# A hybrid diffusion layer on one core: fewer constant matmuls, the second row between the first tiles, filter transfers on another queue, filter steps ahead of the columns

## The chip, the cores and the metric

The kernel runs on one NeuronCore of a Trainium2 chip. A core has five engines that run side by side, each with its own queue, in order: TensorE (PE, matrix multiply, its weight loads shown apart as PEld), VectorE (DVE), ScalarE (ACT), GpSimd (POOL) and SyncE (SP, which here only starts DMA transfers). Matmuls write to PSUM; everything else lies in SBUF. The metric is the device time of one execution in microseconds, lower is better, as the median of several runs. The profile and the trace come from one more, profiled execution.

## The reference, cut to what matters

One layer over 256 latent tokens and 256 context tokens of width 2048, all in float32:

```python
mod   = (silu(c)     @ w_ada + b_ada)      # 9 chunks of 2048: shift, scale, gate for three sub-layers
mod_c = (silu(c_ctx) @ w_ada + b_ada)
x   = half_ffn(x,   mod,   0, g0, w_up1, w_dn1)    # x + 0.5 * gate * swiglu(rms_norm(x) * (1+scale) + shift)
ctx = half_ffn(ctx, mod_c, 0, g0, w_up1, w_dn1)
h, hc = modulated norms of x, ctx                  # then one input projection
attn = attention(q, [kc; k], [vc; v])              # 8 query heads, 2 key heads
hyo  = hyena(h @ w_hy, filters)                    # short conv, gate, long convolution by rfft/irfft, gate
x = x + gate * (concat(rms_norm(attn), rms_norm(hyo)) @ w_out)
x = half_ffn(x, mod, 2, g2, w_up2, w_dn2)
```

The long filter of the Hyena group depends on weights alone: a small three-layer sine network over 256 positions, `h = sin(freq * (z @ w + b))` three times, then `h @ w4` times `exp(-t * abs(decay))`, forward and backward halves, normalised by the sum of absolute values, and its Fourier transform.

## The kernel before, in words

Tokens lie along the free axis: `xs[i]` holds stream i (0 latent, 1 context) as 16 blocks of 128 features by 256 tokens. A matmul in float32 accuracy is made of three faster ones: each operand is split in a high part `hi` (ACT, a cast) and a low part `lo` (DVE, the difference), and `mm3` (L231 to L234) adds hi x hi, lo x hi and hi x lo. `Ffn.tile` does this for one block k of features and one feed-forward tile j of 128 gate and 128 up columns: six matmuls of 128x512.

The change lies in the start of the program, before the main loop of the first feed-forward. It has these parts.

**Norm sums.** The 16 loads of x come first on SP's queue. ACT squares them (L594), DVE adds them up (L255), and PE sums over the features with matmuls against ones (L607, four matmuls of two columns each for a group). Around these stand constant matmuls, `keep_awake` (L578, `ones` times `pair`, 128x256, results unused): `AWAKE[0]` of them ahead of the first group of sums and `AWAKE[3]` between the first group and the rest. PE takes them in this order. Then follow the root (L262 to L271), a matmul that spreads the reciprocal root over the partitions (L297) and its copy into `rs`.

**Rows and columns of the conditioning.** Shift and scale of the first sub-layer are made for one block d of 128 features at a time. `row_load(d)` loads 2 MB of `w_ada1` as two tiles `wrow` of 1 MB (four buffers, so two rows); `ada_row(d)` is 16 matmuls of 256 columns (L175, 32 records in the trace); `ada_col(d)` copies the row to SBUF (ACT, L182, tile `sg`), turns it (PE, L184) and reduces it to a column (DVE, L187 to L190). Then `wave_h(d)` makes the modulated block `h[d]` in both parts: DVE L648, ACT L650 (hi), DVE L652 (lo); for d = 0 and 1 it is `wave_h_early` (DVE L628, ACT L635, DVE L638, L640).

**The wave.** As soon as `h[d]` is there, it is used for three feed-forward tiles at once (`WAVE = 3`, j = 0, 1, 2), which stay open in PSUM over all 16 blocks. A step d of the loop (L708) is: the row of block d+1, the tile of j = 0, the transposes of row d+1, the tiles of j = 1 and 2. The up weights of the wave come as 512 KB pieces of four blocks; `weights_on` (L686) casts the next pieces when d % 4 = 3 (L221, L225), and POOL's queue loads the ones after (L721 is a copy that gates them, L723 the loads). The first pieces are loaded in two slices, one block (`head`) and three blocks (`rest`), and cast by `first_hi` (ACT, L563) and `first_lo` (DVE, L566).

**Filter steps.** `filter_spectrum` is a generator; the wave calls `next(steps)` once a tile, and what is emitted there has its place in the order of every engine. Three sine layers (PE L436, DVE L438 to L443, ACT L445), then four quarters q of 256 channels. A quarter loads its *taps* (decay, L425, partition-broadcast, and `w4`, L428; 128 KB each, four DMAs), takes the absolute value (ACT L464), exponentials (L468), splits `w4` (ACT L470, DVE L471), multiplies (PE L475, L476), makes sums and norm (DVE L477 to L490, ACT L487, PE L493, L494, DVE L496), transforms (PE L502, DVE L503 to L508) and writes two *spectra* of 256 KB to DRAM (L510). Taps of quarter q+1 are loaded when quarter q begins. Before the change SP's queue carries the taps and the transform matrix (L450), among the rows, and ACT's queue the spectra.

The order of instructions within an engine is made when the program is built, from the order of the calls, their data and `then` / `issue_after`, which put one instruction behind another.

Of the kernel before, what the change touches and what calls it, by code (L numbers as in the profile page):

```python
# [33 lines left out]
FILTER_J = 36  # L34
GATE_J = 20

AWAKE = (32, 0, 0, 14)

QSTEP = (2, 1, 3, 2)
FILL = (2, 0)  # L40
# [15 lines left out]
def hybrid_layer_kernel(ctx: ExitStack, tc: tile.TileContext, a):  # L56
# [26 lines left out]
    def PB(shape=(P, 512)):  # L83
        return T(pp, shape, "pb")
# [327 lines left out]
    def filter_spectrum():  # L412
# [9 lines left out]
        def load_taps(q):  # L422
            dec, w4 = U((P, 2, L)), U((P, 2, L))
            for fb in range(2):
                nc.sync.dma_start(dec[:, fb, :],  # L425
                                  a["flt_decay"][:, fb * HW + q * L : fb * HW + (q + 1) * L].partition_broadcast(P))
            for r in range(2):
                nc.sync.dma_start(w4[r * NF : (r + 1) * NF],  # L428
                                  a["flt_w4"].rearrange("k (f c) -> k f c", f=2)[:, :, q * L : (q + 1) * L])
            return dec, w4  # L430


        for li in range(3):
            np_ = P if li == 2 else NF
            ps = PB((np_, L))
            PE.matmul(ps, ws[li], hcur, start=True, stop=True)  # L436
            ar, kk = T(up, (np_, L), "mt", bufs=3), T(up, (np_, L), "mt", bufs=3)
            V.tensor_scalar(ar, ps, vecs[0:np_, li : li + 1], vecs[0:np_, 3:4], op0=ALU.add, op1=ALU.mult)  # L438
            V.tensor_scalar(kk, ar, 1.0 / TWO_PI, MAGIC, op0=ALU.mult, op1=ALU.add)
            V.tensor_scalar(kk, kk, MAGIC, None, op0=ALU.subtract)  # L440
            for cst in (RED1, RED2, RED3):
                V.scalar_tensor_tensor(ar, kk, -cst, ar, op0=ALU.mult, op1=ALU.add)
            V.tensor_scalar(ar, ar, 3.1415925, -3.1415925, op0=ALU.min, op1=ALU.max)  # L443
            hcur = U((np_, L))
            S.activation(hcur, ar, AF.Sin)  # L445
            yield
            if li == 0:

                mats = U((P, 2, 2, P))
                nc.sync.dma_start(mats, a["fdft"])  # L450
            if li == 1:
                taps = [load_taps(0)]
            yield
            yield
# [4 lines left out]
        for q in range(4):  # L459
# [29 lines left out]
            V.tensor_add(kts[0], kts[0], kts[1])  # L489
            V.tensor_add(ab, ab, kts[0][:, 1, :])  # L490
            yield
            psn = PB((P, 2, L))
            PE.matmul(psn[:, 0, :], ones, ab, start=True, stop=True)  # L493
            PE.matmul(psn[0:1, 1, :], alt, pm[0][:, 0, :], start=True, stop=True)  # L494
# [4 lines left out]
            for sn in range(2):  # L499
                ps, eo, o = PB((P, 2, L)), kts[sn], now[sn]  # L500
                for t in range(2):
                    PE.matmul(ps[:, t, :], mats[:, sn, t, :], pm[t][:, sn, :], start=True, stop=True)  # L502
                V.tensor_mul(eo, ps, rn.unsqueeze(1).broadcast_to((P, 2, L)))  # L503
                V.tensor_add(o[:, 0, :], eo[:, 0, :], eo[:, 1, :])
                V.tensor_sub(o[:, 1, :], eo[:, sn, :], eo[:, 1 - sn, :])
                if sn:
                    V.tensor_copy(o[0:1, 0, :], now[0][0:1, 1, :])
                    V.tensor_copy(now[0][0:1, 1, :], mid)  # L508
                    for n in range(2):
                        nc.scalar.dma_start(spec[2 * q + n], now[n])  # L510
                yield


# [142 lines left out]


    wave = [f1.open(alt=j >= 2) for j in range(WAVE)]
    head, rest = slice(0, 1), slice(1, 4)
    then(roots[-1], first_hi, 0, head)  # L660
    with tc.issue_after(spread.ins):
        made = [first_hi(j, head) for j in range(1, WAVE)][-1]
# [25 lines left out]
            w[j] = weight(None, (P, 4, 2, P), raw=raws[j])  # L688


    for j in range(WAVE):
        mm = f1.tile(0, 0, w[j], wave[j]) if j == 0 else then(mm, f1.tile, 0, 0, w[j], wave[j])
    with tc.issue_after(shifted.ins), tc.issue_after(lo_last.ins):
        for j in range(2):
            first_hi(j, rest)
            first_lo(j, rest)
        scaled = times_rs(1)
    then(mm, row_on, 1)
    copied, mm, bank = then(scaled, ada_col, 1)
    shifted, lo_last = then(copied, wave_h_early, 1)  # L700
    with tc.issue_after(shifted.ins), tc.issue_after(lo_last.ins):
        first_hi(2, rest)
        first_lo(2, rest)
    with tc.issue_after(lo_last.ins), tc.issue_after(mm.ins):
        next(steps)
    mm = keep_awake(AWAKE[2], mm, bank)

    for d in range(1, KT):  # L708
        if d > 1:
            mm = then(mm, row_on, d + 1) or mm  # L710
        for j in range(WAVE):
            mm = then(mm, f1.tile, d, d % 4, w[j], wave[j])
            if d == 1 and j == 0:
                mm = then(mm, row_on, 2)
            if j == (1 if d == 1 else 0):
                mm = then(mm, col_on, d + 1) or mm
            weights_on(d, j)
            if (d, j) != (1, 0):
                next(steps, None)
        if d % 4 == 1 and d // 4 < 3:  # L720
            gate = G.tensor_copy(warm, mod[0][0][:, d : d + 1])  # L721
            with tc.issue_after(gate.ins):
                raws = [weight_load(f1.wup[j, d // 4 + 1], (P, 4, 2, P), G) for j in range(WAVE)]  # L723
# [719 lines left out]
```

## Time and profile before

| | us |
|---|---|
| median of 3 runs | 2686.22 |
| lowest and highest | 2685.14, 2686.62 |
| the profiled execution's own time | 2686.6 |
| its span (first to last instruction) | 2684.8 |
| granted clock of PE over the span | 0.993 |

| engine | busy us | share of the span |
|---|---|---|
| PE | 2654.8 | 99% |
| PE weight load | 2183.4 | 81% |
| DVE | 1725.7 | 64% |
| ACT | 940.5 | 35% |
| POOL | 6.4 | 0% |

How the rows of the trace are read: in a timeline row stand the start, the time taken, engine, line, operation, tiles (written <- read, without buffer numbers), shape and count, and in brackets how long the engine stood idle before it and what ended that. SPq, ACTq and POOL with `DMA_DIRECT2D` are the issuing of transfers, not the transfers. The granted clock is PE's: 1.00 is full speed, 0.50 half. A matmul's record overlaps the next, so the distance of two starts tells its price. In the list of DMA issues stand the tile, the queue, the count, the size of one and the median time from issue to landing.

### The profile page before, as it was taken

How to read it: one execution, taken by the hardware profiler on the slowest of the kernel's cores; microseconds unless marked ns; L12 is line 12 of the kernel's file. 1: busy time of each engine (PE TensorE's matmuls, PEld its weight loads, DVE VectorE, ACT ScalarE, POOL GpSimd, SP SyncE). 2: the span in 40 equal slices, each digit the busy share in tenths (PEclk: the TensorE clock that was granted, in tenths of full speed). 3: DMA queues.
4: the chain of work that ended last, by engine and by line, in shares of the span. 5: the costliest groups of instructions: out<-in, count | busy, mean ns of one | idle time of the engine just before them, and what ended most of it. 6: DMA issues, size and time to landing. Idle time of an engine off the chain costs nothing.

```text
span 2684.8 us, 32551 instructions
## 1 busy us (share of the span) xinstructions
PE 2654.8 (99%) x12538; PEld 2183.4 (81%) x12538; DVE 1725.7 (64%) x2700; ACT 940.5 (35%) x1238; POOL 6.4 (0%) x19
## 2 busy tenths in 40 slices
PE   9899999999999999999999999999999999999999
PEld 6568888888888888888888888888888888888887
DVE  4669898987587667542434497789765555554444
ACT  3343222222222222222222365457454444444333
POOL 0000000000000000000000000000000000000000
PEclk8899999999999999999999999999999999999999
DMA  8777656566687566633223355435545555556664
GB/s 313 251 286 236 226 209 219 210 229 210 226 276 258 204 229 210 224 120 101 95 95 101 126 169 183 144 110 164 197 160 190 190 188 188 188 189 207 200 203 157
DMA packets 145686, 515.77 MB, mean 192 GB/s; under 512 B 16699, under 2 KB 21756, under 8 KB 141180
## 3 DMA queue, kind: packets, MB, share of 16 engines
q1 hardware_dynamic: 142460, 504.13, 55.1%
q10 hardware_dynamic: 1776, 4.85, 0.5%
q0 software_dynamic: 1296, 4.72, 0.5%
q8 instruction: 98, 1.61, 0.2%
q14 instruction: 56, 0.46, 0.0%
HBM read 509.43 MB, written 4.21 MB: 191 GB/s over the span
## 4 chain that ended last, share of the span: by engine, by line
PE 97%; DVE 1%; ACT 1%; DMA 1%; issue 0%; SPq 0%; POOL 0%; DVEq 0%; ACTq 0%; POOLq 0%
PE pa L232 12%; PE pa L233 12%; PE pa L234 12%; PE pa L1107 10%; PE pa L1106 10%; PE pa L1105 10%; PE pb L232 7%; PE pb L233 7%; PE pb L234 7%; PE pa L240 3%; PE pa L242 2%; PE pb L175 1%; PE pa L819 1%; PE pa L820 1%; PE pa L818 1%; PE pa L578 1%
## 5 line engine op out<-in xcount | busy, mean ns | idle before, releaser
L225 DVE TENSOR_TENSOR wlo<-raw,whi 128x1024 fp32r<-128x1024 f32 x639 | 782.1, 1224 | 643.4 <-ACT whi L221 635.3
L221 ACT CAST whi<-raw 128x1024 fp32r<-128x1024 f32 x639 | 671.0, 1050 | 1338.8 <-PE pa L233 488.8
L232 PE MATMUL pa<-u,whi 128*128 128x512 f32 x1376 | 539.6, 393 | 3.2 <-ACT u L635 3.1
L233 PE MATMUL pa<-u,whi 128*128 128x512 f32 x1376 | 537.8, 391 | 0.4 <-DVE u L640 0.4
L234 PE MATMUL pa<-u,wlo 128*128 128x512 f32 x1376 | 537.1, 390 | 0.0
L1105 PE MATMUL pa<-whi,u 128*128 128x512 f32 x1060 | 414.1, 391 | 0.0
L1106 PE MATMUL pa<-wlo,u 128*128 128x512 f32 x1060 | 413.0, 390 | 0.2 <-DVE wlo L225 0.2
L1107 PE MATMUL pa<-whi,u 128*128 128x512 f32 x1060 | 413.0, 390 | 0.0
L232 PEld LDWEIGHTS pa<-u,whi 128*128 128x128 f32 x1376 | 258.9, 188 | 64.4 <-issue 6.9
L233 PEld LDWEIGHTS pa<-u,whi 128*128 128x128 f32 x1376 | 259.2, 188 | 55.1 <-DVE u L640 1.6
L234 PEld LDWEIGHTS pa<-u,wlo 128*128 128x128 f32 x1376 | 259.2, 188 | 53.9
L232 PE MATMUL pb<-u,whi 128*128 128x512 f32 (+1 forms) x800 | 298.8, 374 | 0.0
L233 PE MATMUL pb<-u,whi 128*128 128x512 f32 (+1 forms) x800 | 297.7, 372 | 0.0
L234 PE MATMUL pb<-u,wlo 128*128 128x512 f32 (+1 forms) x800 | 297.7, 372 | 0.0
L1106 PEld LDWEIGHTS pa<-wlo,u 128*128 128x128 f32 x1060 | 199.1, 188 | 41.4 <-DVE wlo L225 0.6
L1107 PEld LDWEIGHTS pa<-whi,u 128*128 128x128 f32 x1060 | 199.0, 188 | 41.4
L1105 PEld LDWEIGHTS pa<-whi,u 128*128 128x128 f32 x1060 | 199.1, 188 | 40.6
L138 DVE CUSTOM_DVE_ANT_0 adas<-adaw,crow,mod 128x1024 bf16<-128x1024 f32 x160 | 205.2, 1283 | 21.6 <-DMA adaw<-in_w_adaT_dram 18.9
L138 DVE CUSTOM_DVE_ANT_0 adas<-adaw,crow,cond 128x1024 bf16<-128x1024 f32 x160 | 205.0, 1281 | 16.4 <-DMA adaw<-in_w_adaT_dram 14.6
L232 PEld LDWEIGHTS pb<-u,whi 128*128 128x128 f32 x800 | 150.6, 188 | 27.2 <-issue 0.9
L233 PEld LDWEIGHTS pb<-u,whi 128*128 128x128 f32 x800 | 150.7, 188 | 26.3
L234 PEld LDWEIGHTS pb<-u,wlo 128*128 128x128 f32 x800 | 150.7, 188 | 26.2
(279 smaller groups left out, 2151.5 us busy)
## 6 DMA issues: line engine op xcount, KB each, us to landing
raw<-in_w_up_dram SPq DMA_DIRECT2D x340, 512.0 KB, 3.3
adaw<-in_w_adaT_dram SPq DMA_DIRECT2D x223, 512.0 KB, 4.9
raw<-in_w_dn_dram SPq DMA_DIRECT2D x184, 512.0 KB, 3.4
wrow<-in_w_ada_dram SPq DMA_DIRECT2D x32, 1024.0 KB, 7.3
raw<-in_w_hy_dram SPq DMA_DIRECT2D x32, 512.0 KB, 3.3
raw<-in_w_o_dram SPq DMA_DIRECT2D x32, 512.0 KB, 3.5
raw<-in_w_kv_dram SPq DMA_DIRECT2D x16, 512.0 KB, 3.3
raw<-in_w_q_dram SPq DMA_DIRECT2D x16, 512.0 KB, 3.3
```

The source lines that it names most:

```text
L138: V.tensor_tensor_reduce(out=sc, in0=t, in1=crow[i][:, b * (D // 2) : (b + 1) * (D // 2)], scale=1.0, scalar=mcol if b else bada[:, n : n ...
L175: last = PE.matmul(bank[g : g + 32, 0 : 2 * P], cs[:, k, :], t[:, k8, :], start=k < 4, stop=k >= KT - 4)
L221: S.copy(hi, raw)
L225: V.tensor_sub(lo, raw, hi.bitcast(F32))
L232: PE.matmul(ps, w[0], xx[0], start=start, stop=False)
L233: PE.matmul(ps, w[0], xx[1], start=False, stop=False)
L234: return PE.matmul(ps, w[1], xx[0], start=False, stop=stop)
L240: PE.matmul(ps, w[0], x, start=start, stop=stop)
L242: PE.matmul(ps[:, 0, :], w[1], x[:, 0, :], start=False, stop=False)
L1105: PE.matmul(ps[t], hi, w[0], start=start, stop=False)
L1106: PE.matmul(ps[t], hi, w[1], start=False, stop=False)
L1107: last = PE.matmul(ps[t], lo, w[0], start=False, stop=stop)
```

## The change

There are five edits.

1. The table of constant matmuls goes from (32, 0, 0, 14) to (17, 0, 0, 5): 17 ahead of the first sums, 5 between the two groups of sums. The call for the third number is taken out.
2. For d = 0 and 1 the order is written anew. Row 1 now comes after tile j = 0 of block 0, the transposes of row 1 after tile j = 1, and tile j = 2 after those; before, all three tiles came first. The weights' slices are one, one and two blocks (`head`, `second`, `rest`) in place of one and three, and the casts of `second` go between the column of row 1 and the modulation of block 1.
3. The taps and the transform matrix are issued from POOL's queue in place of SP's, and the spectra from POOL's in place of ACT's.
4. In a step of the wave `next(steps)` stands ahead of `col_on` and of `weights_on`, no more behind them.
5. A quarter of the filter has one more `yield`, ahead of its sums (the matmuls with `ones` and `alt`).

From line 489 on the new kernel's lines are one higher, and from the wave on six (L650 is then L651, L510 is L511, L721 is L727).

```diff
-AWAKE = (32, 0, 0, 14)
+AWAKE = (17, 0, 0, 5)
...
             for fb in range(2):
-                nc.sync.dma_start(dec[:, fb, :],
+                nc.gpsimd.dma_start(dec[:, fb, :],
...
             for r in range(2):
-                nc.sync.dma_start(w4[r * NF : (r + 1) * NF],
+                nc.gpsimd.dma_start(w4[r * NF : (r + 1) * NF],
...
-                nc.sync.dma_start(mats, a["fdft"])
+                nc.gpsimd.dma_start(mats, a["fdft"])
...
             V.tensor_add(ab, ab, kts[0][:, 1, :])
             yield
+            yield
             psn = PB((P, 2, L))
...
-                        nc.scalar.dma_start(spec[2 * q + n], now[n])
+                        nc.gpsimd.dma_start(spec[2 * q + n], now[n])
...
-    head, rest = slice(0, 1), slice(1, 4)
+    head, second, rest = slice(0, 1), slice(1, 2), slice(2, 4)
...
-    for j in range(WAVE):
-        mm = f1.tile(0, 0, w[j], wave[j]) if j == 0 else then(mm, f1.tile, 0, 0, w[j], wave[j])
+    scaled = then(lo_last, times_rs, 1)
+    mm = f1.tile(0, 0, w[0], wave[0])
+    mm = then(mm, row_on, 1)
+    mm = then(mm, f1.tile, 0, 0, w[1], wave[1])
+    with tc.issue_after(mm.ins), tc.issue_after(scaled.ins), tc.issue_after(shifted.ins):
+        copied, mm, _ = ada_col(1)
+    with tc.issue_after(copied.ins):
+        made = [first_hi(j, second) for j in range(2)][-1]
+    shifted, lo_last = then(made, wave_h_early, 1)
+    mm = then(mm, f1.tile, 0, 0, w[2], wave[2])
     with tc.issue_after(shifted.ins), tc.issue_after(lo_last.ins):
         for j in range(2):
-            first_hi(j, rest)
-            first_lo(j, rest)
-        scaled = times_rs(1)
-    then(mm, row_on, 1)
-    copied, mm, bank = then(scaled, ada_col, 1)
-    shifted, lo_last = then(copied, wave_h_early, 1)
-    with tc.issue_after(shifted.ins), tc.issue_after(lo_last.ins):
-        first_hi(2, rest)
-        first_lo(2, rest)
-    with tc.issue_after(lo_last.ins), tc.issue_after(mm.ins):
+            first_lo(j, second)
+        made = first_hi(2, second)
+        made_lo = first_lo(2, second)
+    for j in range(WAVE):
+        with tc.issue_after(made.ins), tc.issue_after(made_lo.ins):
+            made = first_hi(j, rest)
+            made_lo = first_lo(j, rest)
+    with tc.issue_after(made_lo.ins), tc.issue_after(mm.ins):
         next(steps)
-    mm = keep_awake(AWAKE[2], mm, bank)
...
+            if (d, j) != (1, 0):
+                next(steps, None)
             if j == (1 if d == 1 else 0):
                 mm = then(mm, col_on, d + 1) or mm
             weights_on(d, j)
-            if (d, j) != (1, 0):
-                next(steps, None)
```

What this makes of the instructions on the engines is shown at three places. The first is DVE at the third sine layer, which falls in step d = 3 of the wave. `pb_595` is the layer's matmul, `pb_628` the turned row of block 5; `wlo` are the low parts of the next weights. Before:

```order
L438 TENSOR_SCALAR mt_597<-pb_595,u_162 128x256
L225 TENSOR_TENSOR wlo_615<-raw_470,whi_614 128x1024
L439 TENSOR_SCALAR mt_598<-mt_597 128x256
L225 TENSOR_TENSOR wlo_625<-raw_472,whi_624 128x1024
L440 TENSOR_SCALAR mt_598<-mt_598 128x256
L442 SCALAR_TENSOR_TENSOR mt_597<-mt_598,mt_597 128x256
L187 TENSOR_REDUCE col_96<-pb_628 128x4
```

And now, where `pb_557` is the matmul and `pb_530` the turned row of block 4:

```order
L187 TENSOR_REDUCE col_96<-pb_530 128x4
L439 TENSOR_SCALAR mt_560<-mt_559 128x256
L188 SCALAR_TENSOR_TENSOR mod_6_83<-col_96,bada_17_95,cond_78 128x2
L440 TENSOR_SCALAR mt_560<-mt_560 128x256
L190 TENSOR_SCALAR mod_6_83<-col_96,cond_78 128x2
L442 SCALAR_TENSOR_TENSOR mt_559<-mt_560,mt_559 128x256
L649 SCALAR_TENSOR_TENSOR sq_579<-u_111,mod_6_83,u_166 128x256
```

The sine's chain has moved from behind the reduction of row 5 to beside that of row 4, one row earlier on DVE; the two weight differences that stood in it now follow it but for one.

The second place is ACT at the same step. `whi` are the casts of the three next weight pieces, u_582 (now u_577) is the high part of block 4, u_606 (now u_568) the third sine. Before:

```order
L221 CAST whi_591<-raw_468 128x1024
L650 ACTIVATE u_582<-sq_584,mod_6_83 128x256 x2
L221 CAST whi_614<-raw_470 128x1024
L464 ACTIVATE u_536<-u_536 128x512
L221 CAST whi_624<-raw_472 128x1024
L182 COPY sg_655<-pb_628 128x256
L445 ACTIVATE u_606<-mt_597 128x256
```

Now:

```order
L464 ACTIVATE u_518<-u_518 128x512
L221 CAST whi_586<-raw_450 128x1024
L221 CAST whi_596<-raw_452 128x1024
L221 CAST whi_606<-raw_454 128x1024
L445 ACTIVATE u_568<-mt_559 128x256
L651 ACTIVATE u_577<-sq_579,mod_6_83 128x256 x2
L457 CAST u_637<-u_568 128x256
L182 COPY sg_655<-pb_610 128x256
```

The high part of block 4 stood behind the first cast; it now stands behind all three casts and the sine. The copy of row 5 stood ahead of the sine and now stands behind it.

The third place is the queue of the spectra. On ACT, before, at the end of quarter 0 and the beginning of quarter 1 (u_674 and u_675 are the taps of quarter 1):

```order
L182 COPY sg_822<-pb_795 128x256
L650 ACTIVATE u_829<-sq_831,mod_6_83 128x256 x2
L510 DMA spec_20_100<-u_537 128x512
L510 DMA spec_19_99<-u_536 128x512
L468 ACTIVATE u_861<-u_674,u_162 128x512
L468 ACTIVATE u_863<-u_674,u_162 128x512
L470 CAST u_865<-u_675 128x512
L464 ACTIVATE u_854<-u_854 128x512
```

On POOL now, from the gate of the third set of weights to the spectra of quarter 2 (u_640 and u_641 are the taps, later the spectra, of quarter 1, u_1070 and u_1071 are the taps of quarter 3):

```order
L727 COPY mod_8_16_93<-mod_6_83 128x1
L209 DMA raw_1101<-in_w_up_dram 128x1024
L209 DMA raw_1103<-in_w_up_dram 128x1024
L209 DMA raw_1105<-in_w_up_dram 128x1024
L511 DMA spec_22_102<-u_641 128x512
L511 DMA spec_21_101<-u_640 128x512
L425 DMA u_1070<-in_flt_decay_dram 128x256 x2
L428 DMA u_1071<-in_flt_w_dram 64x2x256 x2
L511 DMA spec_24_104<-u_843 128x512
```

The spectra have left ACT, and on POOL the last taps stand behind the spectra of quarter 1.

## The prediction

> **What bounds the kernel now.** I read the windows of the trace by stage first, then the timeline of TensorE (PE) to the first feed-forward matmul, then PE's waits in the wave of 16 rows, then the queue that ended each.
>
> ```profile
> 0.00:36.59 36.59, 32.67 (x161) 25.14 (x161) 13.91 (x32) 15.77 (x29) 0.94 (x7) 0.91 0.86 323
> 36.59:50.99 14.40, 12.19 (x61) 7.28 (x61) 7.50 (x17) 3.58 (x6) 1.89 (x4) 0.77 0.50 185
> 50.99:187.50 136.51, 121.62 (x809) 78.07 (x808) 87.55 (x207) 47.92 (x84) 3.61 (x8) 0.91 0.78 287
> 187.50:2684.80 2497.30, 2488.32 (x11511) 2072.89 (x11510) 1616.77 (x2446) 873.26 (x1121) 0.00 (x0) 1.00 0.55 185
> ```
>
> Columns: stretch and length in us, busy time of PE, weight load, DVE, ACT and POOL, granted clock, DMA share, GB/s. From 187.5 us on PE works 2488.3 of 2497.3 us at full clock: no edit lies there, and it only starts earlier or later. The change can win only in the first 187.5 us. PE is busy in the first stretch too, but with what?
>
> ```profile
> 1.25 16.81 PE L578 MATMUL pa<-u,ones 128*128 128x256 f32 x64 [1.25 <-POOL u L91]
> 14.50 0.63 ACT L594 ACTIVATE u<-u 128x512 f32<-128x512 f32 x1 [0.70 <-DMA u<-in_xT_dram]
> 14.91 0.69 DVE L255 TENSOR_TENSOR u<-u 128x512 f32<-128x512 f32 x1
> 17.90 0.95 PE L607 MATMUL pb<-ones,u 128*128 128x2 f32 x8
> 18.71 6.29 PE L578 MATMUL pa<-u,ones 128*128 128x256 f32 x28
> 24.84 2.87 PE L607 MATMUL pb<-ones,u 128*128 128x2 f32 x24
> 27.74 0.16 DVE L262 TENSOR_SCALAR cond<-pb 128x4 f32<-128x4 f32 x1 [12.06 <-PE pb L607]
> 36.59 0.73 PE L232 MATMUL pa<-u,whi 128*128 128x512 f32 x2 [1.85 <-ACT u L635]
> ```
>
> The last squares are ready at 14.91 + 0.69 = 15.6 us, but the 24 records that sum them (L607) stand behind 28 records of constant matmuls and start at 24.84. DVE then waits 12.06 us for PE. Until 27.7 us the constant matmuls set the time.
>
> In the wave PE stands still four times, and each time the clock falls behind it:
>
> ```profile
> 77.00:80.56 3.56, 0.05 (x2) 0.01 (x1) 1.02 (x4) 3.53 (x7) 0.77 (x2) 1.00 1.03 287
> 80.56:85.98 5.42, 5.20 (x37) 2.14 (x37) 3.81 (x9) 1.74 (x3) 0.00 (x0) 0.69 0.96 379
> 99.50:102.81 3.31, 0.42 (x2) 0.00 (x1) 0.82 (x4) 1.89 (x4) 0.00 (x0) 0.94 1.01 314
> 102.81:109.28 6.47, 6.47 (x37) 2.53 (x37) 2.32 (x4) 0.48 (x1) 0.00 (x0) 0.51 0.23 66
> 113.90:119.14 5.24, 0.00 (x2) 0.00 (x1) 5.18 (x10) 2.40 (x4) 0.00 (x0) 0.70 0.08 33
> 119.14:123.80 4.66, 4.66 (x37) 2.14 (x37) 2.17 (x2) 0.00 (x0) 0.00 (x0) 0.60 0.01 4
> 153.90:156.09 2.19, 0.21 (x2) 0.00 (x1) 1.99 (x5) 2.19 (x5) 0.00 (x0) 1.00 1.05 431
> 156.09:162.47 6.38, 5.36 (x36) 2.00 (x37) 4.78 (x9) 1.53 (x2) 0.00 (x0) 0.57 0.96 327
> ```
>
> Standing: 3.51 + 2.89 + 5.24 + 1.98 + 1.02 = 14.6 us. Behind them, time x (1 - clock) is 5.42 x 0.31 + 6.47 x 0.49 + 4.66 x 0.40 + 5.36 x 0.43 = 9.0 us. Together 23.6 us of the 136.5 are lost to the filter steps' waits.
>
> **The constant matmuls (L578): 46 become 22.** 16.81 us / 32 = 0.53 us each in the first group (it begins cold), 6.29 / 14 = 0.45 in the second. The first group of 17 is 34 of 64 records. If the second group's 0.225 us a record is the warm price, the first has about 13 cold records of 0.44, and 34 take 5.7 + 21 x 0.22 = 10.3: it ends near 11.6 us. Eight sums (0.95) and five constant matmuls (2.25) end near 14.8, when the data are almost there (15.6). The 24 sums (2.87) then end at 17.7 instead of 27.7: **-10.0 us**. Bounds: -7.2 if the cold part is twice as long (26 records, so that the sums end at 20.5), -10.8 for 24 x 0.45.
>
> Is what follows ready 10 us earlier? Loads are issued by SP without waiting for PE until the third row, so their landings stand:
>
> ```profile
> L162 SPq DMA_DIRECT2D wrow<-in_w_ada_dram x1: 328/328/328, 10.4 to 10.4; - x1
> DMA to landing us min/median/max: 9.1/9.1/9.1
> ...
> L162 SPq DMA_DIRECT2D wrow<-in_w_ada_dram x1: 328/328/328, 13.8 to 13.8; - x1
> DMA to landing us min/median/max: 13.0/13.0/13.0
> ```
>
> Row 0's second half is in at 19.5 us. It is wanted behind L297, some 4 us after the sums, so near 21.8. Row 1 is in at 26.8 and wanted when tile j=0 ends, some 3 us after 26.6. Both have over 2 us to spare, so the chain from 27.7 to 36.59 moves whole.
>
> **Row 1 between the tiles.** No work is removed: the 32 records of row 1 go ahead of tile j=1, so that j=2 runs while the column is made. The lone wait is this one:
>
> ```profile
> 43.09 1.93 PE L175 MATMUL pb<-wrow,csp 128*32 128x256 f32 x32
> 47.81 1.22 PE L232 MATMUL pa<-u,whi 128*128 128x512 f32 x2 [1.28 <-ACT u L635]
> 50.99 1.36 PE L175 MATMUL pb<-wrow,csp 128*32 128x256 f32 x20
> ```
>
> The stretch 36.59 to 50.99 holds 14.40 - 12.19 = 2.2 us of idling. Tile j=2 (six matmuls, 1.4 us at 0.23) covers part. The slices cut into 1 + 1 + 2 k-tiles add three casts and three subtractions on engines that wait there. I take **-1.4 us**; bounds 0 and -2.2. The call with the table's third number goes too; that number was 0, so it made nothing.
>
> **Taps and spectra on POOL's queue.** What this takes away is ACT's wait for its own queue:
>
> ```profile
> 100.05 0.82 ACTq L510 DMA_DIRECT2D spec<-u  x2
> 100.92 1.33 ACT L468 ACTIVATE u<-u,u 128x512 f32<-128x512 f32 x2 [2.60 <-DVE u L508]
> 149.39 0.81 ACTq L510 DMA_DIRECT2D spec<-u  x2
> 150.30 0.37 ACT L182 COPY sg<-pb 128x256 f32<-128x256 f32 x1 [6.31 <-DVE u L508]
> ```
>
> ACT stands behind the spectrum writes until DVE's L508 (2.60 and 6.31 us); the second and fourth standstills follow. In the new order L468 and L470 of the second quarter stand a row ahead of their matmul: I put them 2 us before it. The six issues per quarter now go through POOL. At what its weight loads cost (1.57 us for three) that is 3.1 us, hidden under a row's mean of 136.5 / 14 = 9.8 us.
>
> New on POOL: the gate copy and the next three weights stand behind spectra and taps. The weights are wanted two rows later, so a few us do not matter. The fourth taps stand behind the second quarter's spectra; ACT's Abs (L464) waits for them in order, and the row's sg copy behind it.
>
> ```profile
> raw<-in_w_up_dram POOLq DMA_DIRECT2D x9, 512.0 KB, 8.4
> u<-in_flt_decay_dram SPq DMA_DIRECT2D x8, 128.0 KB, 7.4
> 76.21 1.57 POOL L209 DMA_DIRECT2D raw<-in_w_up_dram  x3 [0.37 <-ACT u L445]
> 75.43 0.29 DVE L443 TENSOR_SCALAR mt<-mt 128x256 f32<-128x256 f32 x1
> 75.75 0.42 ACT L445 ACTIVATE u<-mt 128x256 f32<-128x256 f32 x1 [2.76 <-DVE mt L443]
> 76.15 0.91 ACT L650 ACTIVATE u<-sq,mod 128x256 fp32r<-128x256 f32 x2
> 77.37 1.28 ACT L468 ACT_TABLE_LOAD   x1
> ```
>
> **Filter step ahead of the columns, one yield more.** The third sine was ready at 75.43 because L443 stood behind row 5's column reduction. Now L443 comes before that reduction, so the table load and both exponentials end before the matmuls of quarter 0: the first standstill goes. What is late next: ACT now has that sine and all three weight casts ahead of L651 of d=4. The third cast can start when d=3 ends, when row 5's L175 (1.93) begins. By the durations of before DVE reaches L443's end, behind one L225 (1.22), some 2.3 us after that; with the sine's 0.42 and L651's 0.91 ACT is done 3.7 us after, of which L175 covers 1.9: a new wait of **1.8 us**. The sums of quarter 1 (third standstill, 5.24) stand a row later behind the same DVE work: no wait. But quarter 2's L475 now stands at the end of d=9, and ACT reaches L468 only after L651 of d=10, which waits for DVE's last spectrum operations and L649, some 3 us from the row's transposes. With half of L651 (0.45), L468 1.33 and L470 0.60 that is 5.4 us, against 2.7 for tiles j=1 and j=2: a wait of **2.7 us**. Loads add perhaps **1.0** at rows 4 and 5, where the queues are full:
>
> ```profile
> 50.00:60.00 10.00, 10.00 (x90) 6.05 (x89) 4.59 (x15) 3.36 (x6) 0.00 (x0) 0.94 1.01 410
> ```
>
> At 410 GB/s a row of 2 MB takes 5.1 us, and rows 2 to 4 with 2.8 MB of weights and taps, 9.1 MB from 30 us, are in at about 52, with row 4 wanted at about 51. I add 1.0 more for the fourth taps. So 6.5 us of waits stay, and half clock behind the two longer at the mean of the four seen, 9.0 / 4 = 2.25: 11.0 in all, and **-12.6 us** of 23.6. Bounds: -23.6 (nothing waits) and 0 (as many new waits as old).
>
> The Trainium skill (TensorE: Matmul & The Clock Gate, "What's actually happening") has the clock halved only after an idle window of about 3.4 us. By it waits of 1.8 and 2.7 us would cost no clock, and the sum would be 4.5 us less. The trace does not agree: behind idling of 1.98 and 1.02 us the clock was 0.57.
>
> **Sum.** -10.0 - 1.4 - 12.6 = -24.0 on the profiled execution's 2686.6 us (span 2684.8 plus 1.8): 2662.6. That run is 0.4 above the median of the runs, so I predict **2662 us**.
>
> **Rivals.**
> - Nothing waits in the wave: -10.0 - 1.4 - 23.6 = -35: 2651. For it: ACT is busy 47.92 of 136.51 us. Against: it works in order, and one late operand holds all.
> - Waits under 3 us leave the clock alone: -28.5: 2658. Against: the 0.57 above. (The rule cited above is this one.)
> - Early loads: the 10 us are waited for at rows 2 to 5, since DMA is at its limit there: -14: 2672. Against: over 2 us to spare at rows 0 and 1, and the deficit counted above is about 1.
> - The waits only change places: -11.4: 2675. For it: a 1 us slip on DVE moves straight to PE in the quarter's sums.
> - Both of these last: about -1.4, no change: 2685.
> - Slower: POOL's queue. If each of three taps lands late for ACT's Abs by four issues (2.1) and 8.4 of landing, uncovered, with the sg copy queued behind, each costs 10.5 + 2.25: 38.3 - 24.0 = +14: 2700. It decides from 24.0 / 3 = 8 us a time. For it: the fourth taps do stand behind a spectrum write that waits for DVE. Against: only that one set does; the second and third are issued rows ahead. The Trainium skill (SBUF — State Buffer, "SBUF: two separate sides") says that DVE's fast copies lock GpSimd out of writing descriptors; that would lengthen just these landings. No trace here shows it.
>
> **How the numbers follow.** Forecast 0.52, nothing waits 0.12, clock spared 0.08, early loads 0.08, waits change places 0.12, no change 0.04, slower 0.04. Less than 0.2% (5.4 us) cannot be told from nothing: faster 0.92, same 0.04, slower 0.04. The range goes from the no-wait case to the changed-places case with a microsecond for the start's bounds: 2651 to 2676.
>
> **What would show it.** Right: L608's 24 records end near 17.7 us with DVE's wait for them under 3; the first feed-forward matmul near 26.6; row 2's L175 near 39.6; PE's wait before the first L475 gone, one under 2 us before d=4 and one of 2 to 3 before quarter 2's L475; ACT with no wait for L509; the last row done near 163 us. Wrong: PE waiting for wrow loads, L464 or sg waiting long for taps, or idle time on PE behind 190 us.

## The result: 2658.65 us, and the profile after

The changed kernel took 2658.65 us, the median of 5 runs (2658.15 to 2661.81), against 2685.14 for the kernel before (5 runs, 2683.43 to 2686.62): a ratio of 0.9905, 95% interval 0.9891 to 0.992. That is faster, 3.4 us below the forecast of 2662 and inside its range of 2651 to 2676. The profiled execution spans 2656.9 us against 2684.8, so 27.9 us are to be found. One of the ten runs of row1_only below was slow (4462.51 us, granted clock 0.555): its median of 2684.53 counts that run, its interval does not, and the other nine have 2684.29.

The windows of the changed kernel, cut at the same events as the prediction's: the first feed-forward matmul, row 2's first L175, the first matmul of the tile behind the wave. The columns are the stretch and its length, busy time of PE, weight load, DVE, ACT and POOL, granted clock, DMA share, GB/s.

```profile
0.00:27.41 27.41, 21.68 (x112) 15.05 (x112) 13.90 (x32) 15.74 (x28) 0.95 (x7) 0.88 0.95 360
27.41:38.93 11.52, 10.67 (x60) 6.03 (x60) 4.99 (x14) 3.94 (x9) 0.87 (x2) 0.85 0.99 393
38.93:160.12 121.19, 113.25 (x809) 75.22 (x809) 88.75 (x214) 49.85 (x87) 19.13 (x35) 0.99 0.89 324
160.12:2656.90 2496.78, 2487.82 (x11511) 2072.78 (x11509) 1615.25 (x2446) 871.82 (x1118) 0.00 (x0) 1.00 0.55 185
```

The start lost 36.59 - 27.41 = 9.2 us, the stretch with row 1 14.40 - 11.52 = 2.9, and from row 2 to the end 15.8 went (2684.8 - 50.99 = 2633.8 against 2656.9 - 38.93 = 2618.0). The tile behind the wave began at 187.75 us before, so the last stretch was 2497.05 us and is as long now to 0.3. The wave itself, from 50.99 to 187.75 and now from 38.93 to 160.12, went from 136.8 to 121.2 us. In it PE's idle time fell from 15.0 to 7.9 us, and its busy time from 121.8 to 113.3 although its instructions are the same: that second part is clock.

PE's timeline at the start (start, length, engine, line, tiles, count; in brackets the idle time before it and what ended it):

```profile
1.25 9.06 PE L579 MATMUL pa<-u,ones 128*128 128x256 f32 x34 [1.25 <-POOL u L91]
11.40 1.05 PE L608 MATMUL pb<-ones,u 128*128 128x2 f32 x8 [1.09 <-DVE u L255]
15.45 3.08 PE L608 MATMUL pb<-ones,u 128*128 128x2 f32 x24 [0.73 <-DVE u L255]
27.41 0.73 PE L232 MATMUL pa<-u,whi 128*128 128x512 f32 x2 [1.85 <-ACT u L636]
```

PE now waits for DVE's sums of squares, where DVE had waited 12 us for PE. The sums end at 15.45 + 3.08 = 18.5 us instead of 27.7.

All waits of over 0.5 us that PE has left in the wave, and the first load wait:

```profile
52.49 1.07 PE L175 MATMUL pb<-wrow,csp 128*32 128x256 f32 x16 [0.45 <-DMA wrow<-in_w_ada_dram]
61.27 1.07 PE L175 MATMUL pb<-wrow,csp 128*32 128x256 f32 x16 [1.35 <-DMA wrow<-in_w_ada_dram]
68.58 1.72 PE L175 MATMUL pb<-wrow,csp 128*32 128x256 f32 x28 [0.55 <-DVE u L477]
102.28 1.93 PE L175 MATMUL pb<-wrow,csp 128*32 128x256 f32 x32 [1.58 <-DVE mt L498]
111.96 0.73 PE L475 MATMUL pb<-u,u 128*128 128x512 f32 x2 [2.35 <-ACT u L470]
113.95 3.35 PE L175 MATMUL pb<-wrow,csp 128*32 128x256 f32 x32 [0.55 <-DVE u L477]
156.36 0.50 PE L233 MATMUL pa<-u,whi 128*128 128x512 f32 x1 [1.03 <-DVE u L653]
```

They sum to 7.9 us. Only behind the 2.35 does a row of the wave run slow: the L175 at 113.95 takes 3.35 us for the 1.93 of the one at 102.28. The four standstills of before (3.51, 2.89, 5.24, 1.98 + 1.02) are gone from their places.

### The profile page after: what moved, and what is told of

It is laid out like the page before. It is cut to its first block, busy times and chain, and to the rows that moved or that the text cites. A ratio compares the mean times of both kernels' runs of the same rounds, so it can differ in the third digit from the quotient of the medians.

```text
span 2656.9 us, 32472 instructions
## 1 busy us (share of the span) xinstructions
PE 2633.4 (99%) x12490; PEld 2169.1 (82%) x12490; DVE 1722.9 (65%) x2703; ACT 941.4 (35%) x1241; POOL 20.9 (1%) x44
## 4 chain that ended last, share of the span: by engine, by line
PE 93%; DVE 1%; ACT 0%; issue 0%; ACTq 0%; DVEq 0%
PE pa L233 11%; PE pa L234 11%; PE pa L232 11%; PE pa L1111 10%; PE pa L1112 10%; PE pa L1113 10%; PE pb L232 7%; PE pb L233 7%; PE pb L234 7%; PE pa L240 3%; PE pa L242 2%; PE pa L825 1%; PE pa L826 1%; PE pa L824 1%; PE pb L1268 0%; PE pb L1051 0%
```

## Experiments

Twelve kernels ran. To compare them, each profiled execution is cut at the same places: the start of the first feed-forward matmul, the time from it to row 2's first L175, and the time from there to the end of the span. The last column counts the half-clock windows behind row 2, stretches in which PE's granted clock was 0.50. Each was 3.41 us long, or two on end, and a window filled with work cost 1.71 us. The kernel before was timed again beside each group of runs (medians 2684.05 to 2685.33), and the ratio is to that; medians of different groups can differ by a microsecond for this alone.

| kernel | median us | ratio to before, 95% | first matmul | to row 2 | row 2 to end | windows |
|---|---|---|---|---|---|---|
| before | 2685.14 | | 36.59 | 14.40 | 2633.8 | 7 |
| changed | 2658.65 | 0.9891 to 0.992 | 27.41 | 11.52 | 2618.0 | 1 |
| constants_only | 2678.0 | 0.9965 to 0.9984 | 27.22 | 14.92 | 2634.1 | 7 |
| row1_only | 2684.53 | 0.9985 to 1.0005 | 36.59 | 11.67 | 2636.2 | 8 |
| queues_only | 2684.17 | 0.9989 to 1.0007 | 34.76 | 13.14 | 2634.2 | 6 |
| steps_only | 2669.22 | 0.9923 to 0.9956 | 35.46 | 14.38 | 2618.2 | 1 |
| queues_undone | 2661.13 | 0.9892 to 0.9925 | 28.03 | 11.36 | 2621.0 | 2 |
| yield_undone | 2661.05 | 0.9897 to 0.9927 | 27.40 | 12.45 | 2622.8 | 2 |
| yield_twice | 2660.51 | 0.9893 to 0.9923 | 26.84 | 11.82 | 2618.6 | 1 |
| one_constant | 2662.24 | 0.99 to 0.993 | 30.17 | 11.69 | 2618.7 | 1 |
| yield_both | 2654.49 | 0.987 to 0.9903 | 26.23 | 10.19 | 2614.4 | 1 |
| idle_filled | 2659.05 | 0.9888 to 0.9918 | 27.72 | 12.30 | 2616.6 | 0 |
| late_filter_loads | 2654.62 | 0.9874 to 0.9904 | 27.98 | 12.17 | 2612.6 | 0 |
| both_queues_undone | 2654.06 | 0.9871 to 0.9904 | 27.57 | 11.38 | 2612.4 | 0 |

The last four columns are of one execution each. The first matmul starts up to 1.8 us apart with the same table (34.76 to 36.59 with the old one, 26.23 to 28.03 with the new one), so single differences of a microsecond or two say nothing by themselves.

### Each edit alone

The table of constants (constants_only):

```
-AWAKE = (32, 0, 0, 14)
+AWAKE = (17, 0, 0, 5)
```

> The kernel before with the table (17, 0, 0, 5) alone. Theory (a start that ends earlier passes whole): the sums L607 end near 18.5 us as in the changed kernel, the first feed-forward matmul is near 27.4 instead of 36.6, and all four standstills of the wave stay: -9.2, about 2676. Rival (the loads eat it): PE waits for wrow loads at rows 2 to 5 about as long as it began earlier: -2 or less, 2683 or more.

Measured 2678.0, -7.3 by the medians and -8.6 by the span. PE's timeline shows the start moved and the standstills left alone:

```profile
27.22 1.22 PE L232 MATMUL pa<-u,whi 128*128 128x512 f32 x2 [1.86 <-ACT u L635]
71.98 0.50 PE L475 MATMUL pb<-u,u 128*128 128x512 f32 x1 [3.51 <-ACT u L470]
94.29 0.79 PE L475 MATMUL pb<-u,u 128*128 128x512 f32 x1 [2.89 <-ACT u L470]
110.67 1.22 PE L493 MATMUL pb<-u,ones 128*128 128x256 f32 x2 [5.24 <-DVE u L490]
```

No L175 waits for a load, and the time from row 2 to the end is that of before (2634.1): the wave takes nothing of what the start gains. Of the 9.4 us in this trace, 0.5 are lost in the stretch with row 1 (14.92 us). The rival of the loads falls for this edit.

Row 1 between the tiles (row1_only):

```
-    for j in range(WAVE):
-        mm = f1.tile(0, 0, w[j], wave[j]) if j == 0 else then(mm, f1.tile, 0, 0, w[j], wave[j])
+    mm = f1.tile(0, 0, w[0], wave[0])
+    mm = then(mm, row_on, 1)
+    mm = then(mm, f1.tile, 0, 0, w[1], wave[1])
...
```

With it go the slices 1, 1, 2 and the order of casts that belong to them.

> The kernel before with row 1 between the first tiles and the weight slices 1, 1, 2 alone. Theory: the stretch from the first feed-forward matmul to row 2 falls from 14.4 to near 11.5 us (its two half-clock windows become one), and nothing behind it changes: -2.9, about 2682. Rival: what row 2 starts earlier is waited for in the wave: within 1 us of before.

Measured 2684.53, no change by its interval. In the trace the stretch did shrink by 2.7 us (row 2's L175 starts at 48.26 instead of 50.99), and the wave then took 2.4 longer. The waits in it are those of before to 0.35 us. It has one half-clock window more, 1.7 us: its first standstill, 3.64 us, had two windows behind it (78.5 to 85.5 us), that of before, 3.51 us, one. So most of what was lost later is one window more in this execution. The interval, -4.0 to +1.3 us, holds -2.7 and 0 alike: the runs do not separate the two answers, only the stretch itself is shown.

Taps and spectra on POOL's queue (queues_only):

```
-                nc.sync.dma_start(dec[:, fb, :],
+                nc.gpsimd.dma_start(dec[:, fb, :],
...
-                        nc.scalar.dma_start(spec[2 * q + n], now[n])
+                        nc.gpsimd.dma_start(spec[2 * q + n], now[n])
```

The other half of the taps and fdft go the same way.

> The kernel before with taps and spectra on GpSimd's queue alone. Theory (ACT's wait for its own spectrum writes makes the second and fourth standstill): the 2.89 at 99.9 us and the 1.98 + 1.02 at 154 us go, with the half clock behind them (about 4.8 in four windows of which most goes), the 3.51 and the 5.24 stay: -8 to -10, about 2676. Rival (DVE's spectrum operations are late themselves, ACT's wait only shows it): the same four standstills, -0 to -3, 2683 or more.

Measured 2684.17 (10 runs, interval -3.0 to +1.9 us): the rival's number, though not for its reason alone. PE's waits:

```profile
63.94 1.07 PE L175 MATMUL pb<-wrow,csp 128*32 128x256 f32 x16 [2.72 <-DMA wrow<-in_w_ada_dram]
80.32 0.79 PE L475 MATMUL pb<-u,u 128*128 128x512 f32 x1 [3.50 <-ACT u L470]
100.56 0.73 PE L475 MATMUL pb<-u,u 128*128 128x512 f32 x2 [0.18 <-ACT u L470]
114.45 1.22 PE L493 MATMUL pb<-u,ones 128*128 128x256 f32 x2 [5.25 <-DVE u L490]
153.32 0.73 PE L475 MATMUL pb<-u,u 128*128 128x512 f32 x2 [1.98 <-ACT u L470]
```

The second standstill did go (2.89 to 0.18), but a load came 2.72 us late for row 4. That wait belongs to this edit: all eight traced kernels with the taps and fdft on POOL's queue wait 0.69 to 2.96 us for loads of rows 4 or 5, and none of the six without does. (That the early taps and fdft are what delays the row is borne out below, where loading them later shortens the wait.) And the fourth standstill stayed at 1.98, with ACT free of its spectrum writes. ACT's timeline there:

```profile
149.68 0.91 ACT L650 ACTIVATE u<-sq,mod 128x256 fp32r<-128x256 f32 x2 [0.47 <-DVE sq L648]
150.50 1.04 ACT L221 CAST whi<-raw 128x1024 fp32r<-128x1024 f32 x1
151.44 1.33 ACT L468 ACTIVATE u<-u,u 128x512 f32<-128x512 f32 x2
152.67 0.60 ACT L470 CAST u<-u 128x512 fp32r<-128x512 f32 x1
```

L468 stands behind L650 and a cast, and these behind DVE, as before. The 6.31 us that ACT had waited for its queue lay ahead of other waits.

Filter steps ahead of the columns, with the added yield (steps_only):

```
+            if (d, j) != (1, 0):
+                next(steps, None)
             if j == (1 if d == 1 else 0):
                 mm = then(mm, col_on, d + 1) or mm
             weights_on(d, j)
-            if (d, j) != (1, 0):
-                next(steps, None)
```

(and the second `yield` before a quarter's sums)

> The kernel before with the filter step ahead of a row's columns and the added yield alone. Theory: the first (3.51) and the third standstill (5.24) go with the half clock behind them (1.7 and 3.2): -10 to -13; the second and fourth stay or move, since ACT still waits for its spectrum writes: about 2674. Rival (without the queues the order only moves the waits): ACT's writes hold the quarter behind them as long as before and PE stands elsewhere: -0 to -4, 2682 or more.

Measured 2669.22, -16.1: more than the theory gave, and the time from row 2 to the end, 2618.2, is that of the whole change (2618.0). All four standstills went with this edit:

```profile
72.08 0.73 PE L232 MATMUL pa<-u,whi 128*128 128x512 f32 x2 [0.82 <-ACT u L651]
112.75 1.93 PE L175 MATMUL pb<-wrow,csp 128*32 128x256 f32 x32 [1.81 <-DVE mt L498]
122.47 0.51 PE L475 MATMUL pb<-u,u 128*128 128x512 f32 x1 [2.33 <-ACT u L470]
167.09 0.50 PE L233 MATMUL pa<-u,whi 128*128 128x512 f32 x1 [1.03 <-DVE u L653]
```

These are the waits of the changed kernel, but for the loads and the 0.82. ACT still writes spectra and still waits for DVE between the two L468 of quarter 1, as its timeline shows, and PE does not notice, though with nothing to spare: L470 ends at 97.53 us and PE's L475 starts at 97.58.

```profile
95.43 0.81 ACTq L511 DMA_DIRECT2D spec<-u  x2
96.30 0.72 ACT L468 ACTIVATE u<-u,u 128x512 f32<-128x512 f32 x1 [2.34 <-DVE u L509]
96.93 0.60 ACT L470 CAST u<-u 128x512 fp32r<-128x512 f32 x1
97.58 0.50 PE L475 MATMUL pb<-u,u 128*128 128x512 f32 x1
```

By the traces the four parts add up, each counted in its own stretch: -9.4 at the start, -2.7 with row 1, 0 (+0.4) for the queues, -15.6 in the wave, together -27.3 to -27.7 of the 27.9. By the medians they are -7.3, -0.8, -1.2 and -16.1, together -25.4 of 26.5.

### One part of the changed kernel undone

The queues back to SP and ACT, everything else as changed:

> The changed kernel with taps and fdft back on SP's queue and the spectra back on ACT's. Theory (the order of the steps alone took all four standstills, so the queues bring nothing): within 2 us of the changed kernel, 2657 to 2661, no standstill before L475 of quarters 1 and 3, and PE's waits for wrow loads at rows 4 and 5 (1.8 us) smaller. Rival (the prediction's: ACT behind its spectrum writes holds L468): 2 to 3 us before L475 of quarters 1 and 3 each and one or two half-clock windows of 1.7 us behind each: 2664 to 2670.

Measured 2661.13 (4 runs, 2659.41 to 2662.19), 2.5 above the changed kernel; the runs of the two overlap. There is no standstill before L475 of quarters 1 and 3, so the theory holds. Rows 4 and 5 find their loads, and another wait stands there instead:

```profile
63.52 0.73 PE L232 MATMUL pa<-u,whi 128*128 128x512 f32 x2 [1.88 <-ACT u L651]
113.81 0.80 PE L475 MATMUL pb<-u,u 128*128 128x512 f32 x1 [2.36 <-ACT u L470]
```

The 1.88 before d=4 is the wait that the prediction had put at 1.8. In the changed kernel row 5's late load (1.35) covers it. Of the 3.0 us that the wave of this execution is longer, 1.7 is a second half-clock window behind the 2.36.

The added yield alone taken out:

> The changed kernel without the added yield. Theory (the yield alone took the third standstill, the wait of quarter 1's sums for DVE's L490): 3 to 5 us before L494 of quarter 1 and two half-clock windows of 1.7 us behind it: 2664 to 2667. Rival (the step ahead of the columns is enough, since L490 then stands ahead of the row's column reduction): within 2 us of the changed kernel.

Measured 2661.05 (2659.95 to 2664.38). My theory was wrong: PE does not stand before the sums of quarter 1, so the order ahead of the columns had already taken the 5.24 (queues_only still has 5.25 there). The longest waits of this trace, with 1.51 us before an L184 and 0.95 before an L175 beside them:

```profile
63.25 1.13 PE L175 MATMUL pb<-wrow,csp 128*32 128x256 f32 x16 [2.96 <-DMA wrow<-in_w_ada_dram]
90.42 0.73 PE L475 MATMUL pb<-u,u 128*128 128x512 f32 x2 [2.30 <-ACT u L470]
```

The load wait of 2.96 lies ahead of the first place where the yield acts, so it is not the yield's doing. The 2.3 us before an L475 stand at quarter 1 now, and quarter 2's are gone. The yield moved that wait by a quarter; whether it is worth the 2.4 us between the medians is not settled by these runs.

The constants down to one (one_constant):

```
-AWAKE = (17, 0, 0, 5)
+AWAKE = (1, 0, 0, 0)
```

> The changed kernel with the table (1, 0, 0, 0): no constant matmuls but one. Theory (the data set the sums' end, near 18.5 us, and the constants only hold the clock): the sums come at half clock and the start ends up to 3 us later, 2658 to 2662. Rival (constants still in the way of the sums): the start ends about 1 us earlier, 2657 to 2658, and the 24 records of the sums keep their 3.08 us.

Measured 2662.24, 3.6 above the changed kernel. The sums come late and slow, as the theory had it:

```profile
12.09 1.87 PE L608 MATMUL pb<-ones,u 128*128 128x2 f32 x8 [9.62 <-DVE u L255]
16.00 5.28 PE L608 MATMUL pb<-ones,u 128*128 128x2 f32 x24 [2.04 <-DVE u L255]
```

The sums take 1.7 to 1.8 times as long (5.28 us for the 3.08 of the changed kernel, 1.87 for 1.05), so the constants are worth some 3 us: too many held the sums, one alone leaves them slow. That it is the clock is argued: the granted clock does not show it (last section).

### The wait that is left, and a faster version

The 2.3 us came back each time at another quarter. With 8 steps a quarter and 3 tiles a row, each quarter begins a tile earlier in its row than the last, and one of the three positions is bad. One more yield before quarter 1's sums:

```
             yield
             yield
+            if q == 1:
+                yield
```

> The changed kernel with one more yield, before quarter 1's sums alone, so that everything behind it stands a tile later. Theory (PE's 2.35 us before quarter 2's L475 are a tile too few, and the 1.58 before row 9 a sum too close to the row): both go, with the half-clock window behind the first (1.7): -4 to -5.5, 2653 to 2655. Rival (waits change places: what stands later in quarter 2 and 3 collides with other rows): within 1.5 us of the changed kernel.

Measured 2660.51, no gain, as the rival had it. The waits of 1.58 and 2.35, behind quarter 1's sums and before quarter 2's L475, each stood a quarter later, behind quarter 2's sums and before quarter 3's L475 (the two inserted lines shift the numbers: L500 is L498):

```profile
125.92 1.93 PE L175 MATMUL pb<-wrow,csp 128*32 128x256 f32 x32 [1.71 <-DVE mt L500]
135.61 0.73 PE L475 MATMUL pb<-u,u 128*128 128x512 f32 x2 [2.35 <-ACT u L470]
```

So the position decides, not the quarter: by the count of steps, quarter 2 in the changed kernel, quarter 1 with 7 steps (yield_undone) and quarter 3 here all begin at the same tile of a row. Then `if q in (1, 2)`, which keeps the later quarters at the position of quarter 1:

> The changed kernel with one more yield before the sums of quarters 1 and 2, so that a quarter has 9 steps there, three whole rows, and the next begins at the same tile of a row. Theory (a quarter of 8 steps against 3 tiles a row moves a tile ahead each time, and one of three positions is bad: quarter 2 in the changed kernel, quarter 3 with the yield before quarter 1 alone): no wait of 2.3 us before any L475 and no half-clock window in the wave: -2.4 - 1.7 - 0.5 to 1.6: 2653 to 2655. Rival (the waits come back at another quarter or at the end of the wave, where the last spectrum stands later): 2657 to 2661.

Measured 2654.49 (2651.33 to 2656.41, 4 runs), 4.2 below the changed kernel's median, or 3.3 when each is taken against the kernel before as timed beside it. All its runs, and those of the two kernels built on it below, lie below all runs of the changed kernel. No L475 waits 0.3 us or more, nor does d=15 wait any more. One half-clock window is left, behind row 5's load:

```profile
49.86 1.07 PE L175 MATMUL pb<-wrow,csp 128*32 128x256 f32 x16 [0.33 <-DMA wrow<-in_w_ada_dram]
59.39 1.93 PE L175 MATMUL pb<-wrow,csp 128*32 128x256 f32 x16 [2.10 <-DMA wrow<-in_w_ada_dram]
```

On top of it, fdft and the second taps are loaded behind quarter 0's L475 (late_filter_loads):

```
-            if li == 0:
-
-                mats = U((P, 2, 2, P))
-                nc.gpsimd.dma_start(mats, a["fdft"])
...
-            if q < 3:
+            if 0 < q < 3:
                 taps.append(load_taps(q + 1))
...
+            if q == 0:
+                mats = U((P, 2, 2, P))
+                nc.gpsimd.dma_start(mats, a["fdft"])
+                taps.append(load_taps(1))
```

> The kernel yield_both with fdft and the second quarter's taps loaded behind the first quarter's L475 instead of before the wave's fourth row (0.75 MB less ahead of row 5). Theory (PE's 0.33 + 2.10 us before rows 4 and 5 are loads in turn behind each other at some 400 GB/s, where 0.75 MB take 1.9): the two waits fall to 1 us or less together, the half-clock window at 59 to 63 us goes, about -1.4 - 1.7: 2651 to 2652. Rival (ACT is late for d=4 by nearly as much, its Abs having waited for the first taps, so that L232 waits for L651 where the row's load did): a wait of 1 to 2 us before L232 of d=4 and no change, 2654 to 2655.

Measured 2654.62: no change. The load waits fell to 0.69 in all and, as the rival said, others took the place:

```profile
63.09 0.74 PE L232 MATMUL pa<-u,whi 128*128 128x512 f32 x2 [0.82 <-ACT u L653]
66.54 0.50 PE L471 MATMUL pb<-u,u 128*128 128x512 f32 x1 [1.57 <-ACT u L466]
```

(L653 is L651 of the changed kernel, L471 its L475.) This wave shows no half-clock window and is 1.8 us shorter in its one trace; the medians do not show it.

Then yield_both with the queues back on SP and ACT (both_queues_undone):

> The kernel yield_both with taps and fdft back on SP's queue and the spectra back on ACT's. Theory (the queues bring nothing once the steps stand right): within 2 us of yield_both, 2653 to 2656, with a wait of 1 to 2 us for L651 before d=4 in place of the wait for row 5's load. Rival (ACT's wait for its spectrum writes holds some quarter): a wait of 2 us or more before an L475 or an L651 behind a spectrum, 2657 to 2661.

Measured 2654.06 (2653.1 to 2654.76), level with yield_both, with 1.44 us before d=4 in place of the late load. The theory holds: the queues bring nothing in this version either.

Last, the clock by itself: four constant matmuls go into the wait of 2.35 us of the changed kernel (idle_filled).

```
                 ps, ht = PB((P, 2, L)), hid[:, t * P : (t + 1) * P]
+                for _ in range(4 if (q, t) == (2, 0) else 0):
+                    PE.matmul(ps[:, 0, :], ones, pair, start=True, stop=True)
```

> The changed kernel with four constant matmuls into the bank of quarter 2's first L475, ahead of it, some 1.8 us of the 2.35 that PE waits there. Theory (the clock is halved for 3.41 us where PE works under about half of such a window): the window behind it keeps full clock, -1.7: about 2657, and the 2.35 us of waiting split into constants and 0.5 of waiting. Rival (the clock follows something else, or the constants hold the bank and so delay L475): the half-clock window stays, 2658 to 2660.

Measured 2659.05: no gain in time that these runs show (the changed kernel's go from 2658.15 to 2661.81). The trace decides what the clock did:

```profile
110.64 1.89 PE L476 MATMUL pb<-u,ones 128*128 128x256 f32 x8
113.10 0.73 PE L477 MATMUL pb<-u,u 128*128 128x512 f32 x2 [0.56 <-ACT u L470]
115.09 1.93 PE L175 MATMUL pb<-wrow,csp 128*32 128x256 f32 x32 [0.55 <-DVE u L479]
```

L476 is the constants, L477 the L475 of before. L175 behind them takes 1.93 us, not 3.35. The wave is 1.4 us shorter, and this execution spent four half-clock windows at its start where the changed kernel's spent three.

## Why the prediction was right, and where it was not

**The start.** Forecast -10.0, measured -9.2, within its bounds, and the difference is smaller than that between single traces of the same start (1.8 us). Eight sums stand 1.09 us and 24 sums 0.73 us for DVE, whose last squares came 0.4 us later than assumed, and the 24 took 3.08 instead of 2.87. The step "the chain from 27.7 to 36.59 moves whole" held: PE waited for no load before row 4.

**Row 1.** Forecast -1.4 (bounds 0 and -2.2), measured -2.9 in the trace, -2.7 alone, outside its bounds. The term was mis-sized: it counted the idle time of the stretch, 2.2 us, and not the clock. Idle time did fall by 1.4, from 2.2 to 0.85. But the clock stood at 0.77 over the 14.40 us of before and at 0.85 over the 11.52 now, a loss of 3.3 us against 1.7, which the sum left out. Over all traces the stretch took 13.1 to 14.9 us in the old order and 10.2 to 12.5 in the new.

**The wave.** Forecast -12.6, measured -15.8, of which 15.6 lie in the wave. The waits were to fall by 8.1 us (14.6 to 6.5), and PE's idle time fell by 7.1 (15.0 to 7.9). The half clock was to fall by 4.5 (9.0 to 4.5), and PE's busy time fell by 8.5: seven half-clock windows became one. So the mis-sized term is the half clock, by 4.0 us.

- *Quarter 2's L475*, forecast 2.7: measured 2.35, at that place and for that reason. ACT's L651 of d=10 waits for DVE's L649 behind the last spectrum operations, and L468 and L470 follow it:

```profile
109.27 0.91 ACT L651 ACTIVATE u<-sq,mod 128x256 fp32r<-128x256 f32 x2 [4.56 <-DVE sq L649]
```

- *The new wait before d=4*, forecast 1.8: it is real (1.88 with the queues undone, 0.82 in steps_only), but in the changed kernel row 5's load is late by 1.35 at the same place and covers it. Loads were forecast at 1.0 and measured at 1.8.
- *The fourth taps*, forecast 1.0: nothing. ACT did stand 3.81 us for them, and PE reached nothing that needed ACT in that time.
- *Not foreseen*: 1.58 us before row 10, behind L498 of quarter 1; 1.03 in d=15 behind L653; twice 0.55 behind L477.

**The cause was put in the wrong place.** The step that failed is "Taps and spectra on POOL's queue. What this takes away is ACT's wait for its own queue ... the second and fourth standstills follow". The waits of ACT were there. For the second standstill the step held: with the queues alone it went from 2.89 to 0.18, but the same edit brought a load wait of 2.72. For the fourth it failed: the 1.98 + 1.02 stayed (1.98 + 1.06). Alone the queues brought no time that the runs show, undone they cost 2.5 us by the medians, with runs that overlap, and with the quarters at a good position their removal left 2654.06 against 2654.49. The step order with its yield, alone, took all four standstills. A chain read back to one long wait on an engine does not say that the wait decides: at the fourth standstill L650, a cast and DVE stood behind it and were as late without it. The forecast time did not depend on which edit takes which standstill, since the change holds them all; that it came out in spite of this is luck.

**The clock.** The prediction weighed the Trainium skill (TensorE: Matmul & The Clock Gate, "What's actually happening") against the 0.57 behind 1.98 + 1.02 us, and let the trace decide. Both held in part. These are windows of the changed kernel, then of idle_filled, cut at the edges of a half-clock window or whole windows away from it (behind the stretch stand its length and PE's busy time; the clock is the third number from the right):

```profile
99.85:103.27 3.42, 1.84 (x24) 1.04 (x27) 3.39 (x7) 0.00 (x0) 0.91 (x2) 1.00 1.01 341
103.27:106.68 3.41, 3.41 (x33) 2.41 (x25) 0.34 (x2) 0.37 (x1) 0.00 (x0) 1.00 1.06 389
110.09:113.50 3.41, 1.45 (x4) 0.59 (x4) 1.58 (x4) 1.82 (x4) 1.94 (x4) 1.00 0.95 378
113.50:116.92 3.42, 2.97 (x30) 1.38 (x32) 2.69 (x7) 1.15 (x2) 0.00 (x0) 0.51 0.40 123
```

```profile
111.96:115.38 3.42, 2.31 (x15) 0.97 (x17) 1.72 (x3) 1.08 (x2) 1.20 (x3) 1.00 0.94 328
115.38:118.79 3.41, 3.41 (x41) 2.08 (x34) 1.95 (x6) 1.76 (x4) 0.00 (x0) 1.00 0.71 175
```

Where PE worked 1.84 of 3.42 us the next window kept full clock, where it worked 1.45 of 3.41 the next ran at half. The free-running window of about 3.4 us that the Trainium skill gives on the same page agrees with the 3.41 measured; a wholly idle one is not needed, a wait of 2.35 us was enough. The mean of 2.25 us per wait that the sum used was worked out behind longer standstills: in the waves of these runs a wait of 1.98 us or more was followed by one or two whole windows of up to 1.71 each (in one case, the 2.72 in queues_only, by none), and a wait of 1.88 us or less by none.

**The rivals.** "Waits under 3 us leave the clock alone", 2658, came nearest in time and was given 0.08; its mechanism holds for all waits left but the longest. Early loads, places changed and POOL's queue are out. PE's idle time in the wave fell to about half. The loads wait 1.8 us, and by the runs above that comes from the queues and not from the earlier start. POOL's busy time in the wave rose from 3.6 to 19.1 us, but PE never waited for POOL there. The decay taps took longer to land (median 15.0 us against 7.4), but 5.4 in queues_only, with the same queue: a slower landing by POOL's queue as such does not show.

**The signs.** Those for right came as said (DVE's wait for the sums 2.49 us, row 2 at 38.9 instead of 39.6, no wait before the first L475, ACT not waiting for L509), but for the wait before d=4; the wave's last row was done at 160 us, not 163. Of those for wrong, two showed as well: PE waited 0.45 and 1.35 us for wrow, and L464 waited 3.03 and 3.81 us for taps. The first cost its 1.8 us; behind the 3.81 PE stood for nothing.

## What to carry to other kernels

Where steps of a side task are dealt out over the tiles of a row, count steps per block against tiles per row: if they do not divide, each block sits at another position, and a wait that is cured at one block can come back at the next. Before an edit is credited with a standstill, ask what would end it if the wait named by the profile were gone; here that edit alone was worth nothing that the runs show, and the place of one call in a loop, with one yield, was worth 16 us. In these runs a wait of TensorE of 2 us or more mostly cost a clock window too, so such a wait may be worth splitting; filling it kept the clock in the one trace, but no gain in time was shown.

## What the runs showed of the hardware

Over the 14 traces, of 34 windows of 3.41 us at full clock in which PE worked half the time or less, 31 were followed by one at half clock; of 37 with a share of 0.51 to 0.72, 6. The cut may be off by some tenths of a microsecond (cut slightly otherwise, the counts are 30 of 33 and 7 of 39), so the exact rule stays open. A load wait of 2.72 us (queues_only) was one of the three that cost no window.

The place of the windows differs between executions, also of kernels that start alike, and so does the price of a wait: 2.35 us cost one window in the changed kernel, 2.36 two in queues_undone. The kernel before lost 18.8 us to half clock in its profiled execution, the changed one 6.8.

At the very start the granted clock may not tell the speed. In one_constant it reads 1.00 (third number from the right) while the 24 sums take 5.28 us, 1.7 times their 3.08, with PE busy throughout:

```profile
16.00:21.28 5.28, 5.28 (x28) 1.00 1.02 402
```
